# VectorE multiplies inverse sums by the gate and GpSimd applies the product; B's bias split and W_out's low parts are placed anew

## The chip, the cores and the metric

The kernel runs on one core of one Trainium2 chip. The metric is the device time of one execution in microseconds; the kernel before has a median of 1867.32 us over three runs (1866.57 to 1867.34). The engines are named as the profile names them: PE is TensorE (PEld its weight loads), DVE is VectorE, ACT is ScalarE, POOL is GpSimd, SP is SyncE, whose queue issues the DMAs.

## The reference, cut to what matters

The input is 2048 tokens of 1024 channels. One layer: an adaLN-modulated RMSNorm, one input projection, three groups of attention heads (A: 6 heads of latent attention with rotary keys; B: 5 heads over a band of chunks with a relative-position bias; C: 5 heads with a forget-gate bias), a SiLU gate on each group's output, one output projection, a gated residual and a last RMSNorm.

```
p = softmax(where(mask, s, NEG))          # s: scaled scores, plus B's or C's bias
o = p @ v                                 # per head
y = concat([a_out * silu(a_gate), b_out * silu(b_gate), c_out * silu(c_gate)]) @ w_out
x = x + gate * y
out = rmsnorm(x, final_g)
```

Everything around the change is in this form: for each head and block of 512 queries, the unnormalised output `sum exp(s) v`, the sum of the exponentials, its inverse, and the SiLU gate have to be multiplied together.

## The kernel before, in words

The tokens are worked in two halves of 1024. A half starts with a stage of projections (`stage_lv`), then runs sixteen heads in a fixed order (`order`, B0, B1, ... A5), each over two blocks of 512 queries. Values are kept to more than one fp32r term: most operands come as a high part (a copy by ACT) and a low part (a subtraction by DVE or POOL), and a product takes three matmuls.

**A tile of attention** is 128 keys by up to 512 queries. `scores` runs three matmuls into a PSUM bank `st`, and ACT takes three exponentials of it (`ph` L755, `p` L756, and `st` in place L758). `parts` lets DVE form the low part `pl = st - ph` (L764), and POOL add `p` to the running sum `acc` (L769; four buffers of `p`). `values` runs the two matmuls with `ph` and `pl` into `pv` (L778, L779), three tiles later (`LAG`).

**The end of a block** (64 of them) is `end`, `sums` and `gate`. In `end` ACT copies `pv` to `ob` (L784) and its other 64 rows to `oa` (L786); POOL adds the two halves (L787, `oa`) and multiplies `oa` by the gate `sg` (L788). `sums`, queued to come one tile step later, transposes `acc` on PE (L797), sums it on DVE (L798) and inverts it (L800, `rs`). `gate`, three steps after `end`, spreads `rs` over 512 columns with four PE transposes into a PSUM bank of the tag `mx` (L806), and DVE multiplies that bank by `oa` into `oo` (L808), which SP stores (L809). The tag `mx` has two banks and also serves the matmuls that find row maxima (L959, L970, L1040). The SBUF tag `oo` has two buffers, shared by `ob`, `oo` and the `y` of the output projection.

**The fill of a head** is a list of units that is spread over the steps of the head before it. For a B head, `bias_load` loads `te`, `tb32` and `c8`; `bias` scales them on POOL (L896 `c8`, L899 `tb32`, L900 `te`) and then makes `te`'s high part on ACT (`teh`, L903) and its low part on POOL (`tel`, L904). `evac` takes the projected queries and keys out of PSUM, ACT and DVE in turn (ACT L911, L912, L915, L916; DVE L913, L914), which frees the two banks of the tag `pj`. B0 is the first head of each half; its projections are `made` before, in the projection stage, and its fill runs at once, followed by the gate projection G0. The other eight B heads (B1 to B4 in each half) have sixteen projection units in their fill.

**The output projection** needs W_out as high and low parts in `wo`, which takes the place of the normalised input `hT` when the last gate projection has read it. `load_wo(k)` runs eight times in the second half: a 512 KB load, ACT's high part (L1063), and the low part (L1064) by DVE for even k and POOL for odd k, 128x1024 each. `out_units` then runs in the fills of the last heads.

**The order of the work.** Program order is a priority only. The framework that builds the program gives each engine an order by its own estimate of when an instruction is ready, and sets the waits between engines; each engine then runs its queue in that order and stands at the first instruction that isn't ready.

Of the kernel before, what the change touches and what calls it, by code (L numbers as in the profile page):

```python
# [8 lines left out]
F32 = mybir.dt.float32  # L9
# [4 lines left out]
ALU = mybir.AluOpType  # L14
# [47 lines left out]
def kernel(ctx: ExitStack, tc: tile.TileContext, a: dict, out: bass.AP):  # L62
    nc = tc.nc
    V, A, G, T = nc.vector, nc.scalar, nc.gpsimd, nc.tensor
    dma = nc.sync.dma_start
# [8 lines left out]
    def pst(tag, bufs=2):  # L74
        return ps.tile([128, 512], F32, tag=tag, name=tag, bufs=bufs)
# [4 lines left out]
    def wr():  # L80
        return wrp.tile([128, 1024], F32, tag="wr", name="wr", bufs=3)
# [179 lines left out]
    raw = wr()  # L261
# [466 lines left out]
    def body_units(pool, kind, tb, par, scale, qk, V_of, sg_of, dst):  # L728

        if kind == "B":  # L730
            js = [j for j in range(max(0, 4 * tb - 4), 4 * tb + 4)]
            full = 4 * tb - 1 if tb else 0
            js.remove(full)
            js = [full] + js
        else:
            js = list(range(4 * tb + 4))
        box = {}
        o0, o1 = 64 * par, 64 * par + 64
        i0, i1 = 64 - o0, 128 - o0

        def scores(n):
            j = js[n]
            d = j - 4 * tb
            if d >= 0:
                v0, v1 = 128 * d, 512
            elif kind == "B":
                v0, v1 = 0, 128 * (d + 5)
            else:
                v0, v1 = 0, 512
            c0, c1 = v0, v1  # L750
            st = pst("st", 3)
            qk(st, j, c0, c1)
            p32 = pool.tile([128, 512], F32, tag="acc" if n == 0 else "p32", name="p32", bufs=2 if n == 0 else 4)
            ph = pool.tile([128, 512], F32R, tag="ph", name="ph", bufs=PB)
            A.activation(ph[:, v0:v1], st[:, v0:v1], AF.Exp, scale=scale)  # L755
            A.activation(p32[:, v0:v1], st[:, v0:v1], AF.Exp, scale=scale)  # L756

            A.activation(st[:, v0:v1], st[:, v0:v1], AF.Exp, scale=scale)  # L758
            box[n] = (st, p32, ph, c0, c1)

        def parts(n):
            st, p32, ph, c0, c1 = box[n]
            pl = pool.tile([128, 512], F32R, tag="pl", name="pl", bufs=PB)
            V.tensor_tensor(pl[:, c0:c1], st[:, c0:c1], ph[:, c0:c1].bitcast(F32), op=ALU.subtract)  # L764
            if n == 0:
                box["acc"] = p32
            else:
                acc = box["acc"]
                G.tensor_tensor(acc[:, c0:c1], acc[:, c0:c1], p32[:, c0:c1], op=ALU.add)  # L769
            box[n] = (ph, pl, c0, c1)  # L770

        def values(n):
            if n == 0:
                box["pv"] = pst("pv", 1)
            pv = box["pv"]
            ph, pl, c0, c1 = box.pop(n)
            vt = V_of(js[n])
            T.matmul(pv[:, c0:c1], lhsT=vt, rhs=ph[:, c0:c1], start=n == 0, stop=False)  # L778
            T.matmul(pv[:, c0:c1], lhsT=vt, rhs=pl[:, c0:c1], start=False, stop=n == len(js) - 1)  # L779

        def end():
            pv = box["pv"]
            ob = pool.tile([128, 512], F32, tag="oo", name="ob", bufs=2)
            A.activation(ob, pv, AF.Copy)  # L784
            oa = pool.tile([128, 512], F32, tag="oa", name="oa", bufs=2)
            A.activation(oa[o0:o1, :], ob[i0:i1, :], AF.Copy)  # L786
            G.tensor_tensor(oa[o0:o1, :], oa[o0:o1, :], ob[o0:o1, :], op=ALU.add)  # L787
            G.tensor_tensor(oa[o0:o1, :], oa[o0:o1, :], sg_of()[o0:o1, :], op=ALU.mult)  # L788
            box["oa"] = oa


        def sums():
            acc = box["acc"]
            tp = pst("mx")
            s4 = pool.tile([128, 4], F32, tag="s4", name="s4")
            for t in range(4):
                T.transpose(tp[:, 128 * t:128 * t + 128], acc[:, 128 * t:128 * t + 128], ident)  # L797
            V.reduce_sum(s4, tp.rearrange("p (j k) -> p j k", j=4), axis=AX.X)  # L798
            rs = box["rs"] = pool.tile([128, 4], F32, tag="rs", name="rs")
            V.reciprocal(rs, s4)  # L800

        def gate():

            rb = pst("mx")
            for t in range(4):
                T.transpose(rb[:, 128 * t:128 * t + 128], box["rs"][:, t:t + 1].to_broadcast([128, 128]), ident)  # L806
            oo = pool.tile([128, 512], F32, tag="oo", name="oo", bufs=2)
            V.tensor_tensor(oo[o0:o1, :], rb[o0:o1, :], box["oa"][o0:o1, :], op=ALU.mult)  # L808
            dma(out=dst[o0:o1, :], in_=oo[o0:o1, :])  # L809

        return [(lambda n=n: scores(n), lambda n=n: parts(n), lambda n=n: values(n)) for n in range(len(js))], end, [sums, gate]

    QB, PB, LAG = 3, 3, 3
# [42 lines left out]
    class BCHead:  # L856
# [37 lines left out]
        def bias(self):  # L894
            pool, te, tb32, c8 = self.pool, self.te, self.tb32, self.c8
            G.tensor_scalar(c8, c8, 8.0, 0.0, op0=ALU.mult, op1=ALU.add)  # L896

            G.memset(tb32[:, 0:384], 0.0)
            G.tensor_scalar(tb32[:, 384:640], tb32[:, 384:640], 8.0, c8, op0=ALU.mult, op1=ALU.subtract)  # L899
            G.tensor_scalar(te, te, 8.0, c8, op0=ALU.mult, op1=ALU.subtract)  # L900
            teh = pool.tile([128, 512], F32R, tag="teh", name="teh", bufs=2)
            tel = pool.tile([128, 512], F32R, tag="tel", name="tel", bufs=2)
            A.activation(teh[:, 0:256], te, AF.Copy)  # L903
            G.tensor_tensor(tel[:, 0:256], te, teh[:, 0:256].bitcast(F32), op=ALU.subtract)  # L904
            self.teh, self.tel = teh, tel
# [22 lines left out]
        def fill(self, mid, made=None):  # L928

            grp = f"Q{self.kind}{self.h}"  # L930
            units = [] if made else [lambda: self.tiles.used(grp)]
            if self.kind == "B":
                units.append(self.bias_load)
            for n, b in enumerate(self.blocks):
                pb = made[n] if made else {}
                if not made:
                    units += proj_feat_units(self.hT, lambda: self.tiles.get(grp), b - 2 * self.half, pb)
                if n == 0 and self.kind == "B":
                    units.append(self.bias)
                units.append(lambda b=b, pb=pb: self.evac(b, pb["p"]))  # L940
                if n == 0:
                    units.append(self.load_old)
                    units += mid
            return units

        def max_units(self, b):
# [30 lines left out]
        def qk(self, b, st, j, c0, c1):  # L977
            k1, k2 = self.kb[j // 4]
            q1, q2 = self.qb[b]
            ks = slice(128 * (j % 4), 128 * (j % 4) + 128)  # L980
            d = j - 4 * b
            T.matmul(st[:, c0:c1], lhsT=k2[:, ks], rhs=q2[:, c0:c1], start=True, stop=False)  # L982
            if self.kind == "C":
                if d >= 0:
                    T.matmul(st[:, 128 * d:128 * d + 128], lhsT=ident_b, rhs=mt, start=False, stop=False)
            elif d >= -1:

                r0, r1 = max(128 * d, 0), min(128 * d + 256, 512)
                s0 = r0 - 128 * d
                T.matmul(st[:, r0:r1], lhsT=ident_r, rhs=self.teh[:, s0:s0 + r1 - r0], start=False, stop=False)  # L990
                T.matmul(st[:, r0:r1], lhsT=ident_r, rhs=self.tel[:, s0:s0 + r1 - r0], start=False, stop=False)
            T.matmul(st[:, c0:c1], lhsT=k1[:, ks], rhs=q1[:, c0:c1], start=False, stop=True)  # L992
# [67 lines left out]
    def load_wo(wo, k):  # L1060
        raw = wr()
        dma(out=raw, in_=a["w_out"][128 * k:128 * k + 128, :])
        A.activation(wo[:, 0, k, :], raw, AF.Copy)  # L1063
        (V, G)[k % 2].tensor_tensor(wo[:, 1, k, :], raw, wo[:, 0, k, :].bitcast(F32), op=ALU.subtract)  # L1064

    def out_units(pool, wo, gate, fg, i):
        b, t, box = i // 4, i % 4, {}
# [97 lines left out]
    for half in range(2):  # L1165
        if half == 0:
            made = stage_lv(0, hT, wt_pool, [h0[0][2:]] + h0[1:], lambda: h0p.__exit__(None, None, None), "QB0")
            small_loads()
            wtp.__exit__(None, None, None)
        else:  # L1170
            with opool("wt", 1) as wt_pool:
                made = stage_lv(1, hT, wt_pool, [], lambda: None, "QB0")
        KB = 4 + 2 * half
        with opool("xx") as pool:
# [40 lines left out]
            else:  # L1215
                box, fg, gate = {}, [], []
# [116 lines left out]
```

## Time and profile before

| what | value |
|---|---|
| median of three runs | 1867.32 us |
| the profiled execution, its own time | 1863.08 us |
| its span (first to last instruction) | 1861.1 us |
| mean granted TensorE clock | 0.983 of full |
| PE busy | 1714.6 us, 92% of the span |
| ACT busy | 1195.3 us, 64% |
| DVE busy | 1132.8 us, 61% |
| POOL busy | 1071.9 us, 58% |

Busy time is an average over stages with different limits. The list of waits says for each engine, line and tile how long the engine sat idle, how often and the longest time, until which instruction. In the timeline a row has its start, its length, the engine, the line, the operation, and in brackets the idle time of its engine just before it with what ended it.

### The profile page before, as it was taken

Reading aid. Unit: us, or ns where it says so; the run is one execution under the profiler, and the core shown is the slowest. Engines: PE = TensorE matmul, PEld = TensorE weight load, DVE = VectorE, ACT = ScalarE, POOL = GpSimd, SP = SyncE. Lnnn points to the kernel's source line nnn. Section 1 sums busy time; section 2 is a strip of 40 time slices with the busy share of each in tenths; the row PEclk is TensorE's granted clock in tenths of the full one; section 3 lists DMA queues with packets and bytes.
Section 4 is the critical chain, followed back from the end, with each engine's and each line's share of the span. In section 5 each row is a group of like instructions: output and inputs, shape, how many; then the busy total and the mean of one; then the engine's idle time right before and its main releaser. Section 6 shows DMA issues by size and latency. Waiting matters only on the chain.

```text
span 1861.1 us, 28271 instructions
## 1 busy us (share of the span) xinstructions
PE 1714.6 (92%) x8835; PEld 1415.7 (76%) x8835; DVE 1132.8 (61%) x2447; ACT 1195.3 (64%) x2574; POOL 1071.9 (58%) x1256
## 2 busy tenths in 40 slices
PE   3899989999999986999899999999999997999997
PEld 2799868778777754999778887777777775877786
DVE  7453547866656587344456667777777776644322
ACT  3552347678768688342357778898998887665611
POOL 1541137568655557340156666777777778787864
PEclk9999989999999999999999999999999998999999
DMA  7514845435223241144933232222332334332243
GB/s 278 166 56 149 223 137 154 124 105 186 73 77 115 63 137 46 58 133 120 249 107 95 82 89 77 75 61 76 91 99 86 88 102 129 95 113 72 71 139 113
DMA packets 139994, 209.83 MB, mean 113 GB/s; under 512 B 18734, under 2 KB 72494, under 8 KB 139764
## 3 DMA queue, kind: packets, MB, share of 16 engines
q1 hardware_dynamic: 139844, 208.03, 37.2%
q8 instruction: 70, 1.15, 0.3%
q14 instruction: 80, 0.66, 0.1%
HBM read 154.05 MB, written 57.38 MB: 114 GB/s over the span
## 4 chain that ended last, share of the span: by engine, by line
PE 41%; ACT 7%; POOL 4%; issue 3%; DVE 3%; DMA 1%; SPq 0%; ACTq 0%; DVEq 0%; POOLq 0%
PE pj L359 5%; PE pj L360 5%; PE pj L361 5%; PE pv L778 3%; PE pv L779 3%; PE st L992 2%; PE st L982 2%; ACT st L758 1%; PE mx L1040 1%; PE mx L959 1%; ACT ph L755 1%; ACT p L756 1%; PE st L1051 1%; PE st L1052 1%; POOL p L769 1%
## 5 line engine op out<-in xcount | busy, mean ns | idle before, releaser
L769 POOL TENSOR_TENSOR p<-p,p 128x512 f32<-128x512 f32 (+3 forms) x516 | 539.7, 1046 | 248.8 <-ACT p L756 206.5
L764 DVE TENSOR_TENSOR pl<-st,ph 128x512 fp32r<-128x512 f32 (+1 forms) x580 | 332.7, 576 | 200.3 <-ACT st L758 191.7
L755 ACT ACTIVATE ph<-st 128x512 fp32r<-128x512 f32 (+1 forms) x580 | 299.3, 516 | 226.8 <-PE st L992 121.6
L758 ACT ACTIVATE st<-st 128x512 f32<-128x512 f32 (+1 forms) x580 | 303.8, 524 | 0.0
L756 ACT ACTIVATE p<-st 128x512 f32<-128x512 f32 (+1 forms) x580 | 297.5, 513 | 0.7
L359 PE MATMUL pj<-hT,whi 128*128 128x512 f32 x544 | 223.5, 411 | 14.0 <-ACT q L916 14.0
L779 PE MATMUL pv<-pl,v 128*128 128x512 f32 (+1 forms) x580 | 213.9, 369 | 22.8 <-DVE pl L764 22.5
L778 PE MATMUL pv<-ph,v 128*128 128x512 f32 (+1 forms) x580 | 215.5, 372 | 10.5 <-ACT ob L784 9.8
L360 PE MATMUL pj<-hT,whi 128*128 128x512 f32 x544 | 216.8, 399 | 0.0
L361 PE MATMUL pj<-hT,wlo 128*128 128x512 f32 x544 | 216.5, 398 | 0.0
L1041 DVE TENSOR_REDUCE pm<-mx 128x1 f32<-128x512 f32 (+2 forms) x240 | 139.7, 602 | 30.0 <-PE mx L1040 28.6
L779 PEld LDWEIGHTS pv<-pl,v 128*128 128x128 f32 x580 | 110.6, 191 | 51.7 <-DVE pl L764 37.2
L778 PEld LDWEIGHTS pv<-ph,v 128*128 128x128 f32 x580 | 110.9, 191 | 39.3 <-ACT ob L784 22.6
L962 DVE TENSOR_REDUCE pm<-mx 128x1 f32<-128x512 f32 (+2 forms) x200 | 116.5, 604 | 33.5 <-PE mx L959 16.3
L787 POOL TENSOR_TENSOR oa<-oa,ob 64x512 f32<-64x512 f32 x64 | 82.7, 1292 | 82.8 <-ACT oa L786 49.7
L359 PEld LDWEIGHTS pj<-hT,whi 128*128 128x128 f32 x544 | 104.4, 192 | 28.5 <-ACT q L916 14.8
L992 PE MATMUL st<-q,k 128*128 128x512 f32 (+1 forms) x340 | 124.1, 369 | 0.7 <-DVE q L723 0.7
L982 PE MATMUL st<-q,k 128*128 128x512 f32 (+1 forms) x340 | 119.7, 352 | 1.4 <-DVE pl L764 1.0
L361 PEld LDWEIGHTS pj<-hT,wlo 128*128 128x128 f32 x544 | 103.6, 190 | 21.6
L360 PEld LDWEIGHTS pj<-hT,whi 128*128 128x128 f32 x544 | 104.2, 192 | 15.8
L1040 PE MATMUL mx<-k,q 128*128 128x512 f32 (+2 forms) x240 | 85.5, 387 | 17.3 <-DVE oo L808 8.9
L359 PE MATMUL pj<-wo,oh 128*128 128x512 f32 x256 | 101.1, 395 | 0.0
(393 smaller groups left out, 4186.6 us busy)
## 6 DMA issues: line engine op xcount, KB each, us to landing
wr<-in_w_in SPq DMA_DIRECT2D x54, 512.0 KB
wr<-in_x SPq DMA_DIRECT2D x34, 512.0 KB
v<-dva SPq DMA_DIRECT2D x36, 256.0 KB
q<-dqa SPq DMA_DIRECT2D x48, 192.0 KB
k<-dka SPq DMA_DIRECT2D x72, 128.0 KB
wa<-in_w_ada SPq DMA_DIRECT2D x16, 512.0 KB
do<-oo SPq DMA_DIRECT2D x64, 128.0 KB
wr<-do SPq DMA_DIRECT2D x128, 64.0 KB
```

What stands on the lines that cost most here:

```text
L359: T.matmul(dst, lhsT=lh, rhs=rh, start=i == 0, stop=False)
L360: T.matmul(dst, lhsT=lh, rhs=rl, start=False, stop=False)
L361: T.matmul(dst, lhsT=ll, rhs=rh, start=False, stop=i == n - 1)
L755: A.activation(ph[:, v0:v1], st[:, v0:v1], AF.Exp, scale=scale)
L756: A.activation(p32[:, v0:v1], st[:, v0:v1], AF.Exp, scale=scale)
L758: A.activation(st[:, v0:v1], st[:, v0:v1], AF.Exp, scale=scale)
L764: V.tensor_tensor(pl[:, c0:c1], st[:, c0:c1], ph[:, c0:c1].bitcast(F32), op=ALU.subtract)
L769: G.tensor_tensor(acc[:, c0:c1], acc[:, c0:c1], p32[:, c0:c1], op=ALU.add)
L778: T.matmul(pv[:, c0:c1], lhsT=vt, rhs=ph[:, c0:c1], start=n == 0, stop=False)
L779: T.matmul(pv[:, c0:c1], lhsT=vt, rhs=pl[:, c0:c1], start=False, stop=n == len(js) - 1)
L982: T.matmul(st[:, c0:c1], lhsT=k2[:, ks], rhs=q2[:, c0:c1], start=True, stop=False)
L992: T.matmul(st[:, c0:c1], lhsT=k1[:, ks], rhs=q1[:, c0:c1], start=False, stop=True)
```

## The change

1. In `end`, POOL no longer multiplies `oa` by the gate. In `gate`, DVE multiplies the spread inverse sums (PSUM) by the gate into `gr`, POOL multiplies `oa` by `gr`, and SP stores `oa` instead of `oo`.
2. The last three operations of `bias` (`teh`, `tel`) become a unit of their own, `bias_split`. For B0 of each half it comes at the end of the fill, behind both `evac`; for the other B heads before the last two projection units of the second block.
3. The low parts of W_out are all formed by POOL.

```diff
@@ body_units, end
             G.tensor_tensor(oa[o0:o1, :], oa[o0:o1, :], ob[o0:o1, :], op=ALU.add)
-            G.tensor_tensor(oa[o0:o1, :], oa[o0:o1, :], sg_of()[o0:o1, :], op=ALU.mult)
             box["oa"] = oa
@@ body_units, gate
-            oo = pool.tile([128, 512], F32, tag="oo", name="oo", bufs=2)
-            V.tensor_tensor(oo[o0:o1, :], rb[o0:o1, :], box["oa"][o0:o1, :], op=ALU.mult)
-            dma(out=dst[o0:o1, :], in_=oo[o0:o1, :])
+            gr, oa = pool.tile([128, 512], F32, tag="oo", name="gr", bufs=2), box["oa"]
+            V.tensor_tensor(gr[o0:o1, :], rb[o0:o1, :], sg_of()[o0:o1, :], op=ALU.mult)
+            G.tensor_tensor(oa[o0:o1, :], oa[o0:o1, :], gr[o0:o1, :], op=ALU.mult)
+            dma(out=dst[o0:o1, :], in_=oa[o0:o1, :])
@@ BCHead.bias
             G.tensor_scalar(te, te, 8.0, c8, op0=ALU.mult, op1=ALU.subtract)
+
+        def bias_split(self):
+            pool, te = self.pool, self.te
             teh = pool.tile([128, 512], F32R, tag="teh", name="teh", bufs=2)
             tel = pool.tile([128, 512], F32R, tag="tel", name="tel", bufs=2)
             A.activation(teh[:, 0:256], te, AF.Copy)
@@ BCHead.fill
             if self.kind == "B":
                 units.append(self.bias_load)
+                if made:
+                    units.append(self.bias)
             for n, b in enumerate(self.blocks):
                 pb = made[n] if made else {}
                 if not made:
                     units += proj_feat_units(self.hT, lambda: self.tiles.get(grp), b - 2 * self.half, pb)
-                if n == 0 and self.kind == "B":
+                if n == 0 and self.kind == "B" and not made:
                     units.append(self.bias)
                 units.append(lambda b=b, pb=pb: self.evac(b, pb["p"]))
                 if n == 0:
                     units.append(self.load_old)
                     units += mid
+            if self.kind == "B":
+                units.insert(len(units) if made else -3, self.bias_split)
             return units
@@ load_wo
-        (V, G)[k % 2].tensor_tensor(wo[:, 1, k, :], raw, wo[:, 0, k, :].bitcast(F32), op=ALU.subtract)
+        G.tensor_tensor(wo[:, 1, k, :], raw, wo[:, 0, k, :].bitcast(F32), op=ALU.subtract)
```

## Rows read from the trace of the kernel before

**Rows 1.** The page, part 1: busy us, share of the span, instructions.

```profile
PE 1714.6 (92%) x8835; PEld 1415.7 (76%) x8835; DVE 1132.8 (61%) x2447; ACT 1195.3 (64%) x2574; POOL 1071.9 (58%) x1256
```

**Rows 2.** Windows: stretch, length, busy us of PE, PEld, DVE, ACT, POOL, clock, DMA.

```profile
1180.00:1520.00 340.00, 327.48 (x1545) 251.78 (x1543) 261.76 (x469) 302.42 (x637) 254.12 (x210) 0.99 0.28 81
...
1524.00:1553.00 29.00, 17.28 (x68) 12.03 (x67) 23.57 (x31) 21.83 (x40) 24.65 (x16) 0.84 0.57 171
```

**Rows 3.** Waits, whole span, SP's own last: total us, times, longest.

```profile
DVE oo L808 <- POOL oa L788: 32.6, 13, 5.9
...
ACT teh L903 <- POOL te L900: 13.1, 3, 6.3
...
PE mx L1040 <- DVE oo L808: 8.9, 5, 2.4
...
SPq L809 <- DVE oo L808: 278.0, 53, 10.8
...
SPq L887 <- POOL tel L904: 19.1, 6, 5.3
```

**Rows 4.** Groups by line and shape: GpSimd's running sums of full tiles.

```profile
L769 POOL TENSOR_TENSOR p<-p,p 128x512 f32<-128x512 f32 x279 | 363.1, 1302 | 119.4 <-ACT p L756 97.4 <-PE pj L361 4.8 <-DVE rs L800 3.5
```

**Rows 5.** Timeline around the end of one block, 1314 to 1320 us.

```profile
1315.95 1.29 POOL L788 TENSOR_TENSOR oa<-oa,sg 64x512 f32<-64x512 f32 x1
...
1317.28 0.68 DVE L808 TENSOR_TENSOR oo<-mx,oa 64x512 f32<-64x512 f32 x1 [2.22 <-POOL oa L788]
...
1318.61 0.50 PE L779 MATMUL pv<-pl,v 128*128 128x512 f32 x1 [1.61 <-DVE pl L764]
...
1319.61 0.60 ACT L755 ACTIVATE ph<-st 128x512 fp32r<-128x512 f32 x1 [0.85 <-PE st L992]
```

**Rows 6.** Timeline, PE: first and last of nine idles behind L808.

```profile
735.67 0.50 PE L779 MATMUL pv<-pl,v 128*128 128x512 f32 x1 [3.02 <-DVE pl L764]
...
1573.83 0.50 PE L1040 MATMUL mx<-k,q 128*128 128x512 f32 x1 [1.58 <-DVE oo L808]
```

**Rows 7.** Timeline, change of halves, 741 to 747 us.

```profile
741.95 1.09 PE L806 MATMUL mx<-c_ident,rs 128*128 128x128 f32 x4 [1.35 <-DVE rs L800]
...
745.24 2.95 ACT L349 ACTIVATE wbhi<-wr 128x1024 fp32r<-128x1024 f32 x3 [2.95 <-POOL oa L788]
...
746.35 0.69 PE L359 MATMUL st<-wbhi,hT 128*128 128x384 f32 x1 [3.31 <-ACT wbhi L349]
```

**Rows 8.** Timeline, start of the heads in each half, ACT and PE.

```profile
242.59 0.59 ACT L915 ACTIVATE k<-pj 64x512 fp32r<-64x512 f32 x1
...
246.75 0.42 ACT L903 ACTIVATE teh<-te 128x256 fp32r<-128x256 f32 x1 [3.57 <-POOL te L900]
...
247.84 0.79 PE L359 MATMUL pj<-hT,whi 128*128 128x512 f32 x1 [7.45 <-ACT q L916]
...
248.43 0.63 PE L360 MATMUL pj<-hT,whi 128*128 128x512 f32 x1
...
253.42 0.39 PE L360 MATMUL pj<-hT,whi 128*128 128x512 f32 x1
...
925.58 0.59 ACT L915 ACTIVATE k<-pj 64x512 fp32r<-64x512 f32 x1
...
929.38 0.42 ACT L903 ACTIVATE teh<-te 128x256 fp32r<-128x256 f32 x1 [3.21 <-POOL te L900]
...
930.47 0.79 PE L359 MATMUL pj<-hT,whi 128*128 128x512 f32 x1 [6.54 <-ACT q L916]
```

**Rows 9.** W_out's low parts: min/median/max ns; waits from 1515 to 1560 us.

```profile
L1064 DVE TENSOR_TENSOR wo<-wr,wo x4: 1225/1779/5193, 1527.4 to 1546.3; 128x1024 fp32r<-128x1024 f32 x4
L1064 POOL TENSOR_TENSOR wo<-wr,wo x4: 2337/2418/3367, 1528.3 to 1546.8; 128x1024 fp32r<-128x1024 f32 x4
...
PE pv L779 <- DVE pl L764: 7.0, 3, 4.9
```

**Rows 10.** The bias's low part on GpSimd: min/median/max ns, first and last start.

```profile
L904 POOL TENSOR_TENSOR tel<-te,teh x10: 722/738/744, 247.3 to 1047.8; 128x256 fp32r<-128x256 f32 x10
```

## The prediction

> **What bounds the kernel now.** I read the busy shares first. PE is busy 92% of the span and no other engine over 64% [rows 1], so time is to be had only where PE stands still. Second, the windows: from 1180 to 1520 us, in the second half's heads, PE is busy 327.5 of 340 us and ACT 302.4 [rows 2]. PE loses 12.5 us there, and ACT, 89% busy, is close behind: a PE idle that goes is worth nearly its length, unless ACT's exponentials then set the pace. Third, the list of waits, looking for waits that the changed lines make [rows 3]: DVE stands 32.6 us in 13 places at L808 until POOL's gate product L788, ACT stands 13.1 us at `teh` until POOL's `te`, and the matmuls of the row maxima wait 8.9 us for L808 to free its `mx` bank. Last, the timeline of PE, to see which of these waits leave PE idle, since only that counts.
>
> **The epilogue.** Instruction counts and shapes stay: one DVE and two POOL products of 64x512 per block, 64 blocks. What changes is the order. Now POOL does L787, often one running sum of 1.30 us [rows 4], then L788 of 1.29 us; DVE stands at L808 with `pl` of later tiles queued behind it. In [rows 5] DVE stands 2.22 us, PE then 1.61 us for `pl`, and ACT 0.85 us for PE. Afterwards DVE's product needs the spread sums and the gate, and both are there earlier; POOL's second product waits for DVE instead. In the timeline of PE I find nine idles of this kind after 700 us, between 3.02 and 1.45 us, together 16.9 us; [rows 6] has the first and the last. Full length is the upper end; the lower end is the ratio at ACT, 0.85/1.61, hence 9.0 us. I take three quarters, 12.7 us, because PE is the fuller engine in rows 2 but not by much. At the change of halves ACT's first weight part waits until 745.24 for L788, the last reader of the gate whose memory it takes; with the change DVE's product, 0.68 us behind the transposes that end at 743.04, is that reader, so ACT starts near 743.8: 1.4 us [rows 7]. The sum is 14.1 us, from 9.0 to 18.3.
>
> What this adds: POOL's product waits for DVE, and behind it on POOL stand the running sums, whose four `p` buffers let ACT go on for four tiles. The store now leaves after POOL, about one product (1.29 us) after DVE's. SP already stands 278 us in total at this store [rows 3], with loads of later heads behind it; a store 1.3 us later would be hidden by loads that run a head ahead, and where POOL was late anyway it isn't later at all. I cost it at nothing; without that cover it would be up to 64 x 1.3 us of load delay, on the path only where a head starts on a load.
>
> **The two starts.** Before each half's heads, PE waits for a `pj` bank that ACT frees with L916. ACT stands at `teh` in between, because POOL's `te` waits for the load of `c8`. L915 ends at 243.18, yet L916 follows `teh` at 247.20; without `teh` it starts there, 4.0 us earlier, and in the second half 926.17 instead of 929.82, 3.6 us earlier [rows 8]. Together 7.6 us. The lower end is half, 3.8 us, if other ScalarE work slides in. After each idle, matmuls are spaced 0.43 us until 253.1, at the 1.2 GHz level, instead of 0.23 at 2.4 GHz [rows 8]; twelve matmuls, so 2.4 us per start. The idles that remain are 3.4 and 2.9 us; one of 3.31 us was followed by the low level [rows 7], one of 3.02 us was not [rows 6]. Between two such rows I count no gain and put 4.8 us on the upper end: 12.4 us.
>
> **The bias's split for the other eight heads** keeps its work, ACT 0.42 us and POOL 0.74 us [rows 8, 10], but comes as the third unit before the end of a fill, so that `tel` has only some projections of cover before the first scores read it. With room in its order it costs nothing; at worst PE waits for one running sum and `tel`, 1.30 + 0.74 = 2.0 us a head [rows 4, 10], 16 us in all. I take an eighth, 2 us: `te` is ready long before, so both can be put in any gap. The next `te` load, which already holds SP 19.1 us behind `tel` [rows 3], will come later too; eight projection units lie between that load and its use, so I cost it at nothing.
>
> **W_out's low parts.** DVE's four take 1.23 to 5.19 us, 10.0 us together, POOL's four 2.4 us each [rows 9]. PE waits 7.0 us for `pl` in that stretch [rows 9], 4.9 of it behind the part of 5.19 us. That goes. POOL gets four more of 2.42 us, 9.7 us, into a stretch in which it is busy 24.65 of 29 us [rows 2]; 4.35 us are free, so POOL falls 5.3 us behind, and the four `p` buffers hold back about that much, 4 x 1.30 us. I take half of the 5.3 us as lost: 7.0 - 2.7 = 4.3 us. The ends are 7.0 - 5.3 - 5.3 = -3.6 us, if later `wr` loads wait as well, and 7.0 + 2.4 = 9.4 us, if a low clock level goes too. The Trainium skill, GPSIMD Engine Reference, section 4.1 on engine selection, advises against two-input elementwise work on GpSimd and puts it at about twice VectorE's time. By that rule the four parts lose 4 x (2.42 - 1.78) = 2.6 us by the medians, and the sum below is 17 us instead of 24; the trace agrees with its direction, but one of DVE's four took 5.19 us beside GpSimd's work, which the rule leaves out.
>
> **The sum** is 14.1 + 7.6 + 4.3 - 2 = 24 us. The profiled execution took 1863.1 us (2.0 us around its span), 4.2 us under the median of 1867.3 us. It becomes 1839 us, and against the median 1843 us.
>
> **The rivals.**
>
> *GpSimd is the limit around W_out.* POOL's order puts the low parts ahead of the running sums; ACT stands for `p`, and PE for ACT. Then that part gives -3.6 instead of 4.3 us, and the late buffers hold up two block ends of the next head, 2 us: 1867.3 - 14.1 - 7.6 + 2 + 3.6 + 2 = 1853 us. For it: POOL is 85% busy there. Against: the loads pace the eight parts. The rule cited above points to this case.
>
> *ScalarE takes over.* At 89% busy [rows 2] ACT may hide most of the epilogue's gain: 4 us of it, the starts 7.6 us, W_out and the split nothing, 1 us at the halves, so 1855 us. Against it: ACT itself idles behind PE in [rows 5].
>
> *The order shifts.* The framework reorders every queue; other small waits of PE take the place of those removed, and only 0 to 3 us remain: about 1866 us.
>
> *GpSimd's queue stops at the gate product: slower.* If the framework places POOL's product early, POOL stands while the sums go through PE, DVE, PE and DVE, at least 1.09 + 0.68 us for the last two [rows 5, 7], with running sums behind it; L808's wait comes back on another engine. It decides from the point where POOL falls four `p` buffers, 5.2 us, behind: then ACT stops. At 0.6 us a block on the path, a third of these 1.77 us, it is 38 us over 64 blocks against the 24 us gained: 1867.3 + 14 = 1881 us. For it: POOL is busy 254 of 340 us [rows 2]. Against: in [rows 5] DVE waited last for POOL and not for the sums, so there nothing would stand.
>
> **How the numbers follow.** Chances: the forecast 0.52, GpSimd around W_out 0.12, ScalarE 0.14, the order 0.09, GpSimd's queue 0.13. About 0.2%, 3.7 us, is what a measurement of this kernel can tell from no change. Faster is 0.52 + 0.12 + 0.14 = 0.78, the same 0.09, slower 0.13. All upper ends together give 18.3 + 12.4 + 9.4 = 40 us, 1827 us; all lower ones 9.0 + 3.8 - 3.6 - 16 = -7 us, 1874 us. For 8 in 10 I take 1829 to 1867 us: it holds the forecast without its last corners, both faster rivals and the case of the order.
>
> **What would show it.** Right: no wait of DVE at the new gate product for POOL, PE's idles of [rows 6] gone, PE's first matmul of the heads 4.0 and 3.6 us nearer to the one before it, no L1064 on DVE, and PE's wait for `pl` near 1550 us gone. Wrong: POOL idle before its product until DVE for more than 0.5 us a block, ACT idle at `p` behind POOL, PE idle at the matmuls with `teh` or `tel`, or PE's idle time unchanged with other names.

## The result, and the profile of the changed kernel

The changed kernel takes 1841.07 us (median of four runs, 1836.47 to 1842.21) against 1866.94 us (1865.56 to 1867.34): a ratio of 0.9867, with an interval of 0.9854 to 0.9881, or 25.9 us less. Forecast were 1843 us and 24 us less. The size is right, and partly by luck: the experiments show two terms that were wrong in opposite directions.

First the page of the changed kernel, part 1 (columns as in rows 1):

```profile
PE 1715.8 (93%) x8835; PEld 1415.0 (77%) x8835; DVE 1125.4 (61%) x2443; ACT 1195.2 (65%) x2574; POOL 1079.8 (59%) x1260
```

Busy times hardly move against [rows 1]: 7.4 us leave DVE and 7.9 come to POOL. The profiled span fell by 20.7 us, to 1840.4 us (the execution's own time is 1842.21 us), so the time came out of idle stretches. The list of waits, SP's own last (columns as in rows 3; the gate product on DVE is now `gr` L807, the product on POOL L808, the running sums' transposes L796, the row maxima L1047):

```profile
ACT teh L906 <- POOL te L900: 10.8, 4, 6.4
...
PE pv L779 <- DVE pl L764: 9.3, 13, 1.8
...
PE mx L796 <- POOL p L769: 9.2, 7, 3.0
...
POOL oa L808 <- PE st L1059: 7.1, 2, 3.6
...
POOL oa L808 <- DVE gr L807: 2.2, 5, 0.7
...
DVE gr L807 <- POOL oa L787: 0.9, 1, 0.9
...
SPq L809 <- POOL oa L808: 358.2, 61, 12.4
```

DVE's 32.6 us of standing at the product [rows 3] are 0.9 us, and POOL's new wait for DVE is 2.2 us in five of 64 blocks. Two more places belong to it, though the list gives them to PE: POOL stands 3.5 us before the products at 474.71 and 724.55, and both times DVE's product ended 0.08 us earlier (473.95 + 0.68, 723.79 + 0.68). That makes 9.3 us in seven blocks. At the second of these POOL had stood 2.77 us before the change too, at the running sum at 726.66, for want of the next `p`. PE's wait for `pl` fell from 22.5 us in 18 places to 9.3 in 13, and the 8.9 us until `oo` freed an `mx` bank [rows 3] are 0.6. New is the third line: PE stands 9.2 us for POOL's running sums, where it stood 2.1 us before. The timeline of the changed kernel has each step:

```profile
243.13 0.79 PE L359 MATMUL pj<-hT,whi 128*128 128x512 f32 x1 [3.45 <-ACT q L919]
243.72 0.63 PE L360 MATMUL pj<-hT,whi 128*128 128x512 f32 x1
...
439.97 1.06 ACT L175 ACTIVATE sq<-wr 128x1024 f32<-128x1024 f32 x1 [4.50 <-DMA wr<-in_x]
...
744.22 0.69 PE L359 MATMUL st<-wbhi,hT 128*128 128x384 f32 x1 [1.99 <-ACT wbhi L349]
...
925.42 0.80 PE L359 MATMUL pj<-hT,whi 128*128 128x512 f32 x1 [2.89 <-ACT q L919]
926.01 0.63 PE L360 MATMUL pj<-hT,whi 128*128 128x512 f32 x1
...
1304.21 0.67 DVE L807 TENSOR_TENSOR gr<-mx,sg 64x512 f32<-64x512 f32 x1
...
1306.77 1.28 POOL L787 TENSOR_TENSOR oa<-oa,ob 64x512 f32<-64x512 f32 x1 [0.83 <-ACT oa L786]
...
1309.27 1.29 POOL L808 TENSOR_TENSOR oa<-oa,gr 64x512 f32<-64x512 f32 x1
...
1510.58 7.06 POOL L1071 TENSOR_TENSOR wo<-wr,wo 128x1024 fp32r<-128x1024 f32 x3
...
1517.58 1.27 POOL L769 TENSOR_TENSOR p<-p,p 128x256 f32<-128x256 f32 x2
...
1518.38 1.00 PE L796 MATMUL mx<-c_ident,p 128*128 128x128 f32 x2 [1.87 <-POOL p L769]
...
1543.54 0.47 PE L796 MATMUL mx<-c_ident,p 128*128 128x128 f32 x1 [3.03 <-POOL p L769]
```

The block end near 1305 us is the plainest case: DVE is through with its product at 1304.88, before POOL has even begun the sum L787. In the old order DVE would have stood until past 1309. At the two starts PE's idle is 3.45 and 2.89 us, where it was 7.45 and 6.54 [rows 8], and at the change of halves 1.99 instead of 3.31 us [rows 7]. From 1510 us on the new cost shows: three low parts of W_out back to back hold POOL for 7.06 us, the running sum stands behind them, and PE waits 1.87 us for it, later 3.03 us.

To compare kernels stage by stage, the table takes a matmul that runs 64 times in every kernel, the transpose of the padded maxima (L722). Its 57th and 63rd run (56 and 62 counted from 0) start at 1480.22 and 1672.26 us before and at 1464.89 and 1652.20 after; W_out lies between them. Each entry is the time between two such runs, in one profiled execution. (Two expectations below call them, loosely, the first sums' transpose of a block end; this is the stretch meant.)

| kernel | to 0 | 0–12 | 12–14 | 14–28 | 28–32 (second start) | 32–48 | 48–56 | 56–62 (W_out) | 62–end |
|---|---|---|---|---|---|---|---|---|---|
| before | 264.8 | 165.0 | 27.3 | 224.5 | 268.6 | 331.9 | 198.1 | 192.0 | 188.8 |
| after | 260.2 | 165.7 | 31.4 | 223.1 | 265.0 | 330.0 | 189.4 | 187.3 | 188.2 |
| after, again | 263.1 | 165.8 | 27.2 | 223.1 | 262.9 | 330.0 | 189.5 | 186.8 | 188.1 |
| epilogue alone | 264.0 | 166.1 | 28.3 | 223.4 | 268.0 | 331.3 | 189.3 | 181.2 | 188.1 |
| bias alone | 259.5 | 167.3 | 27.3 | 225.0 | 264.0 | 331.0 | 198.2 | 192.1 | 188.8 |
| W_out alone | 265.8 | 167.3 | 28.5 | 225.2 | 268.7 | 331.8 | 201.1 | 189.3 | 188.9 |
| after, W_out on both | 261.1 | 165.6 | 28.0 | 223.2 | 261.9 | 330.5 | 189.4 | 182.0 | 188.1 |
| after, W_out on DVE | 262.0 | 165.7 | 28.5 | 223.4 | 263.8 | 330.5 | 189.5 | 182.1 | 188.1 |
| the same again | 262.7 | 166.0 | 28.5 | 223.1 | 266.8 | 330.0 | 189.5 | 180.6 | 188.2 |

Two columns carry most of the gain. 48–56 is 189.3 to 189.5 us in every kernel of the table with the new epilogue and over 198 in the three without it. 56–62 falls into three groups: 192 before, 187 with W_out on POOL, 181 to 182 with the new epilogue and W_out as before or on DVE. "After, again" and "the same again" repeat the program of the row that they follow or name, and so show how far one stage varies by itself: 4.2 us in 12–14, up to 3 us at either start.

### The profile page after: what moved, and what is told of

It is laid out like the page before. It is cut to its first block, busy times and chain, and to the rows that moved or that the text cites. A ratio compares the mean times of both kernels' runs of the same rounds, so it can differ in the third digit from the quotient of the medians.

```text
span 1840.4 us, 28356 instructions
## 1 busy us (share of the span) xinstructions
PE 1715.8 (93%) x8835; PEld 1415.0 (77%) x8835; DVE 1125.4 (61%) x2443; ACT 1195.2 (65%) x2574; POOL 1079.8 (59%) x1260
## 4 chain that ended last, share of the span: by engine, by line
PE 67%; ACT 10%; issue 7%; DVE 6%; POOL 6%; DMA 3%; SPq 0%; ACTq 0%; DVEq 0%; POOLq 0%
PE pj L359 9%; PE pj L361 9%; PE pj L360 9%; PE pv L778 5%; PE pv L779 5%; PE st L999 3%; PE st L989 2%; ACT st L758 2%; PE mx L966 2%; ACT p L756 2%; PE mx L1047 2%; ACT ph L755 2%; PE st L360 2%; PE st L359 2%; PE st L1057 2%
## 5 line engine op out<-in xcount | busy, mean ns | idle before, releaser
L787 POOL TENSOR_TENSOR oa<-oa,ob 64x512 f32<-64x512 f32 x64 | 82.6, 1291 | 68.6 <-ACT oa L786 37.3
L361 PE MATMUL pj<-wo,ol 128*128 128x512 f32 x256 | 100.1, 391 | 0.7 <-POOL ol L1084 0.7
## 6 DMA issues: line engine op xcount, KB each, us to landing
q<-dqa SPq DMA_DIRECT2D x48, 192.0 KB
```

The costliest lines, as they stand in the source:

```text
L361: T.matmul(dst, lhsT=ll, rhs=rh, start=False, stop=i == n - 1)
```

## The experiments

**1. The epilogue alone** (part 1 of the change, in the kernel before):

```diff
-            G.tensor_tensor(oa[o0:o1, :], oa[o0:o1, :], sg_of()[o0:o1, :], op=ALU.mult)
...
-            V.tensor_tensor(oo[o0:o1, :], rb[o0:o1, :], box["oa"][o0:o1, :], op=ALU.mult)
+            V.tensor_tensor(gr[o0:o1, :], rb[o0:o1, :], sg_of()[o0:o1, :], op=ALU.mult)
+            G.tensor_tensor(oa[o0:o1, :], oa[o0:o1, :], gr[o0:o1, :], op=ALU.mult)
```

> The kernel before with the first part of the change alone: DVE multiplies the spread sums by the gate, POOL the output by that; the bias's split and W_out's low parts stay as before. Theory (DVE's wait for POOL was PE's idle, 9 places): about 14 us faster than before, 9 to 18, most of it after 1300 us; the idles of PE behind DVE's product are gone. Rival (ScalarE then sets the pace): 4 to 6 us faster, with ScalarE's busy share near 100% in the second half's heads. Rival (the wait comes back as PE's wait for POOL's running sums): under 4 us faster, PE idle at the transposes of the running sum up by as much as the old idles were.

Measured: 1842.03 us against 1864.69, ratio 0.9878 (0.9863 to 0.9893): 22.7 us, nearly the whole of the change and more than the 9 to 18 us expected. The table puts 8.8 us of it in 48–56 and 10.8 us in 56–62. The windows of these two stretches (columns as in rows 2; the clock is the granted share of 2.4 GHz), first of the kernel before, then of this one:

```profile
1282.13:1480.22 198.09, 189.70 (x893) 146.50 (x892) 152.57 (x275) 175.44 (x373) 149.20 (x124) 0.99 0.30 88
1480.22:1672.26 192.04, 172.50 (x765) 134.93 (x763) 125.72 (x211) 142.75 (x288) 150.49 (x131) 0.96 0.38 113
```

```profile
1281.02:1470.35 189.33, 187.39 (x892) 145.35 (x891) 152.93 (x275) 174.75 (x373) 147.61 (x123) 1.00 0.31 92
1470.35:1651.53 181.18, 168.66 (x765) 132.71 (x763) 122.31 (x212) 142.90 (x288) 151.97 (x132) 0.99 0.40 120
```

The same matmuls (within one) take 2.3 and 3.8 us less time on PE, at a granted clock of 1.00 and 0.99 instead of 0.99 and 0.96; the rest, 6.5 and 7.0 us (8.4 to 1.9, 19.5 to 12.5), is time in which PE was not busy. So up to about 6 of the 19.6 us come by the clock, which fell less once the idles were shorter; a matmul right after an idle also counts longer (0.50 instead of 0.39 us in the timelines below), and the two were not taken apart. And two timelines answer a question on W_out, which this kernel leaves as it was, first that of the kernel before, then this one's:

```profile
1545.68 0.68 DVE L808 TENSOR_TENSOR oo<-mx,oa 64x512 f32<-64x512 f32 x1 [2.94 <-POOL oa L788]
1546.29 5.19 DVE L1064 TENSOR_TENSOR wo<-wr,wo 128x1024 fp32r<-128x1024 f32 x1
...
1552.13 0.80 PE L779 MATMUL pv<-pl,v 128*128 128x512 f32 x1 [4.88 <-DVE pl L764]
```

```profile
1531.24 0.67 DVE L807 TENSOR_TENSOR gr<-mx,sg 64x512 f32<-64x512 f32 x1
1531.84 1.21 DVE L1064 TENSOR_TENSOR wo<-wr,wo 128x1024 fp32r<-128x1024 f32 x1
```

This low part, DVE's fourth, is the one that took 5.19 us before [rows 9]. There it began right behind an L808 that had stood 2.94 us for POOL, and ran beside POOL's own part and running sums; here the product does not stand, and the part takes 1.21 us. So the epilogue alone takes away the 4.9 us of PE that hung on it, and leaves W_out's move nothing to gain there.

**2. The bias alone** (part 2 of the change):

```diff
+                if made:
+                    units.append(self.bias)
...
-                if n == 0 and self.kind == "B":
+                if n == 0 and self.kind == "B" and not made:
...
+            if self.kind == "B":
+                units.insert(len(units) if made else -3, self.bias_split)
```

> The kernel before with the second part alone: the split of the bias into high and low part comes at the end of the first head's fill, and for the other eight B heads two projection units before the end. Theory: 7.6 us come from the two starts (PE's first matmul of each half's heads 4.0 and 3.6 us earlier) and the late split costs 2 us: 5 to 6 us faster than before. Rival (the late split of the other eight heads costs as much as the starts give): 0 to 3 us faster; the 4 us that the changed kernel loses between the heads A0 and B2 of the first half show here too.

Measured: 1855.53 us, ratio 0.9948 (0.9933 to 0.9963): 9.2 us, above the 5 to 6 expected. The table has 5.3 us at the first start and 4.6 at the second. The 2.3 us that 0–12 grew by need not be the late split's: the next kernel, which leaves the bias as it was, has the same 167.3. The timeline of this kernel at the first start:

```profile
243.45 0.50 PE L359 MATMUL pj<-hT,whi 128*128 128x512 f32 x1 [3.45 <-ACT q L919]
243.78 0.39 PE L360 MATMUL pj<-hT,whi 128*128 128x512 f32 x1
```

The idle is the 3.45 us of the changed kernel, but the second matmul takes 0.39 us, not 0.63: the granted clock of the next 6 us is 1.00 (2.4 GHz) here and 0.54 in the changed kernel.

**3. W_out alone** (part 3 of the change):

```diff
-        (V, G)[k % 2].tensor_tensor(wo[:, 1, k, :], raw, wo[:, 0, k, :].bitcast(F32), op=ALU.subtract)
+        G.tensor_tensor(wo[:, 1, k, :], raw, wo[:, 0, k, :].bitcast(F32), op=ALU.subtract)
```

> The kernel before with the third part alone: all eight low parts of W_out on POOL. Theory: PE's 7.0 us of waits for DVE's low part of the scores go and POOL's lag takes back 2.7 us: about 4 us faster. Rival (POOL is the limit there): 4 us slower, with PE waiting for POOL's running sums in that stretch. Rival (the DVE part of 5.19 us was slow only because of POOL at its side, and its removal pays twice): 7 to 9 us faster.

Measured: 1864.01 us, ratio 0.9992 (0.9979 to 1.0004): no change, and none of the three expectations. In its own stretch 2.7 us go; in 48–56, where its work does not lie, 3.0 us come. These are busy time of PE (192.8 instead of 189.7 us) at a granted clock of 0.97 instead of 0.99, with no more idle, in a profiled execution that was the slowest of the ten (1868.51 us). The wait for `pl` behind the 5.19 us part is gone, but its timeline shows what replaces it:

```profile
1535.55 7.04 POOL L1064 TENSOR_TENSOR wo<-wr,wo 128x1024 fp32r<-128x1024 f32 x3 [0.58 <-ACT wo L1063]
...
1543.33 0.33 PE L797 MATMUL mx<-c_ident,p 128*128 128x128 f32 x1 [1.54 <-POOL p L769]
```

**4. The old products, with the gate unit five steps behind the block's end instead of three.** It gives POOL more time, but DVE's product still takes its operand from POOL.

```diff
-                    tail.extend((clock[0] + d, u) for d, u in zip((1, 3), t))
+                    tail.extend((clock[0] + d, u) for d, u in zip((1, 5), t))
```

> The kernel before with one number changed: the unit that spreads the inverse sums and multiplies (DVE) and stores comes five tile steps after a block's end instead of three. No operation changes its engine or order of factors. Theory (only DVE's standing for POOL's gate product costs): POOL is through by then, most of the nine idles go, 8 to 14 us faster than before. Rival (what helps is that DVE's product takes no operand of POOL at all, since POOL lags in any step): less than 4 us faster. Rival (the store or the last block's chain then comes too late): slower by about two tile steps, 4 us, at the ends of the halves.

Measured: 1858.12 us, ratio 0.9957 (0.9940 to 0.9974): 6.6 us, under a third of experiment 1, between the 8 to 14 us of the theory and the rival's 4. Its list of waits:

```profile
PE pv L779 <- DVE pl L764: 28.5, 22, 3.0
DVE oo L808 <- POOL oa L788: 25.8, 9, 5.9
```

DVE still stands 25.8 of the 32.6 us, the longest 5.9 us as before: where it stood longest, two further steps were not enough. Part of the shortfall may be the later store: 62–end is 191.0 us here instead of 188.8. So two steps of slack do not give the epilogue's gain, and an order in which DVE takes no operand from POOL does; more slack was not tried.

**5. The changed kernel, with the later eight B heads splitting right behind the bias**, as before the change; only the starts split late.

```diff
-                    units.append(self.bias)
+                    units += [self.bias, self.bias_split]
...
-            if self.kind == "B":
-                units.insert(len(units) if made else -3, self.bias_split)
+            if self.kind == "B" and made:
+                units.append(self.bias_split)
```

> The changed kernel, with the late split kept only for the first head of each half; the other eight B heads form the low part right behind the bias, as before. Theory (the late split by itself costs the 2 us that the kernel with the split alone lost between the blocks at 313 and 375 us): 1 to 3 us faster than the changed kernel, about 1839 us. Rival (those 2 us come with any order of the first heads and the late split is free): the same as the changed kernel within 1 us, 1841 us.

Measured: 1842.86 us, ratio 0.9881 (0.9856 to 0.9905) to a median before of 1863.98. That is the changed kernel's ratio, with an interval too wide to exclude 2 us by itself. By stretches the late split of these eight costs nothing: outside 12–14 and the starts, which vary by themselves, no stretch of this kernel is over 0.7 us shorter than the changed kernel's (166.4 us in 0–12, 223.4 in 14–28, 331.6, 189.5, 186.6 and 188.0 from 32 on). The rival of this run held.

**6 to 8. W_out put back.** Three kernels from the changed one: low parts on DVE and POOL in turn (6), the same with experiment 5's edit (7), all on DVE (8, `V` in place of `(V, G)[k % 2]`).

```diff
-        G.tensor_tensor(wo[:, 1, k, :], raw, wo[:, 0, k, :].bitcast(F32), op=ALU.subtract)
+        (V, G)[k % 2].tensor_tensor(wo[:, 1, k, :], raw, wo[:, 0, k, :].bitcast(F32), op=ALU.subtract)
```

> The changed kernel with W_out's low parts on DVE and POOL in turn, as before: the first two parts of the change. Theory (with the epilogue rearranged, POOL is late in that stretch and its four extra parts cost what the epilogue's change gained there: 7 us less was won between the blocks at 1480 and 1590 us than with the epilogue alone): about 1834 us, 7 us faster than the changed kernel, with PE's waits for POOL's running sums near 1518 and 1543 us (1.87 and 3.03 us) gone. Rival (those waits only change their names, since DVE's parts then hold up the low part of the scores): 1839 to 1842 us.

> Both: the late split at the two starts alone, and W_out's low parts on DVE and POOL in turn. If both theories hold and add up: 1831 to 1833 us, the fastest so far. If the first falls: like the kernel with W_out on both alone. If the second falls: like the one with the starts alone.

> The changed kernel with all eight low parts of W_out on DVE. Theory (POOL is the limit in that stretch, DVE has room once it stands for nobody): as fast as with both engines or faster, 1832 to 1836 us, each part 1.2 to 1.9 us on DVE. Rival (a DVE part beside POOL's work stretches to several us and holds up the scores' low parts): 1840 us or slower, PE waiting over 5 us more for DVE's low part of the scores between 1500 and 1560 us.

Measured: 1835.35 us, ratio 0.9848 (0.9825 to 0.9870); 1838.80, 0.9860 (0.9839 to 0.9882); 1835.32, 0.9847 (0.9832 to 0.9861). Their 56–62 are 182.0, 182.1 and 182.1 us against 187.3. Experiments 5 and 7 differ in W_out's parts alone: 186.6 against 182.1 us in the stretch, 1842.86 against 1838.80 us in all, with overlapping intervals. So the move of W_out to POOL costs some 5 us in its stretch once the epilogue is changed. Run 7 missed the 1831 to 1833 us expected if both theories held; the first of them had failed in run 5. DVE takes all eight parts in run 8 in the same 182.1 us, though not without a price: PE stands behind three of them in a row (4.22 us from 1508.72), where in run 6 it stands 1.57 us.

```profile
1513.72 0.79 PE L1059 MATMUL st<-q,k 128*128 128x512 f32 x1 [4.35 <-DVE q L723]
```

**9. The squares of x one step later**, in kernel 6. I had put down the 4 us that the changed kernel loses between runs 12 and 14 of L722 to ScalarE's wait for a load of x (4.50 us at 439.97 in the timeline above).

```diff
-                mids[7] = mids.get(7, []) + [lambda t=t: x_norm(load_x(8 + t, wr()), pool.tile([128, D], F32, tag="xn", name="sq", bufs=3),
+                mids[8] = mids.get(8, []) + [lambda t=t: x_norm(load_x(8 + t, wr()), pool.tile([128, D], F32, tag="xn", name="sq", bufs=3),
```

> The changed kernel with W_out's low parts on both engines, and the eight x_norm units of a head put one step later. Theory (the wait of ScalarE's square for the x load, 2.6 us near 440 us in the run with both engines and 4.5 us in the changed kernel, is part of what the first start gained and lost again): no such wait of ScalarE over 1 us, and 1 to 4 us less than with both engines alone, 1831.5 to 1834.5 us. Rival (the wait only moves to the next piece of work that reads the load, or the later units crowd what follows them): 1835 to 1838 us, with a wait of PE in the next 100 us that is not in the other runs.

Measured: 1840.18 us, ratio 0.9874 (0.9855 to 0.9894), 5 us more than kernel 6 (whose interval overlaps) and beyond the rival's 1838. The wait moved, to the next loads of the same kind:

```profile
460.49 1.06 ACT L175 ACTIVATE sq<-wr 128x1024 f32<-128x1024 f32 x1 [3.21 <-DMA wr<-in_x]
...
464.82 0.80 PE L778 MATMUL pv<-ph,v 128*128 128x512 f32 x1 [2.44 <-ACT ob L784]
```

The rival held as to the wait: 14–28 grew from 223 to 230.8 us. Of that, 6.3 us are busy time of PE (221.3 us at a granted clock of 0.96, where the changed kernel's second execution has 215.0 at 1.00). The next run takes the theory's ground away.

**10 and 11. The changed kernel again, and W_out on DVE again, side by side.** The instruction order of these two is the same on every engine up to the loads and parts of W_out, so the 5.7 us between kernel 8 and the result could be the spread of runs.

> The changed kernel as it is, beside the next one on one chip. Theory (W_out's low parts on GpSimd cost about 5 us once the epilogue is changed): 1840 to 1843 us, and 186 to 188 us for the stretch from the first sums' transpose of the 56th to that of the 62nd block end. Rival (the 5.7 us to the kernel with DVE forming them are the spread of runs, since both kernels are the same up to 1530 us): 1836 to 1838 us, within 2 us of the next one.

> The changed kernel with all of W_out's low parts on VectorE, a second time, beside the changed kernel on one chip. Theory: 4 to 6 us under the changed kernel of the same call, 1834 to 1837 us, and 181 to 183 us for the same stretch. Rival: within 2 us of it.

Measured: 1838.72 us, ratio 0.9875 (0.9860 to 0.9890), and 1837.92 us, 0.9866 (0.9850 to 0.9882). By the whole time the two can't be told apart, as the rival had it. By the stretch they can: 186.8 against 180.6 us, as the theory had it, and no kernel with the new epilogue and W_out's parts on DVE or on both lies above 182.1 there, apart from the 184.8 of run 9. What hid it in these two executions is elsewhere: the second start, 262.9 us in the first and 266.8 in the second, in code that is the same. The timeline of the changed kernel's second execution there:

```profile
924.77 0.50 PE L359 MATMUL pj<-hT,whi 128*128 128x512 f32 x1 [2.90 <-ACT q L919]
925.11 0.39 PE L360 MATMUL pj<-hT,whi 128*128 128x512 f32 x1
```

After an idle of 2.90 us the matmuls go on at 0.39 us; in the first execution of the same program, after 2.89 us, at 0.63 (timeline above, 926.01). The trace of run 11 has the low level there as well. The same second execution has 27.2 us in 12–14, as before the change, with a wait of 1.8 us for x instead of 4.5, so the loss of 4 us near 440 us is not fixed to the program. It came in two more executions (30.7 us in 12–14 with a wait of 3.75 us in run 5, 31.1 with 4.15 in run 7); what decides it stays open.

How the cost of W_out on POOL divides shows in the windows of 56–62, of the changed kernel's two executions and of run 11:

```profile
1464.89:1652.20 187.31, 173.34 (x765) 135.59 (x764) 116.99 (x208) 143.18 (x288) 158.17 (x136) 0.95 0.38 116
...
1461.62:1648.45 186.83, 171.96 (x764) 134.78 (x763) 117.01 (x208) 143.08 (x288) 158.21 (x136) 0.96 0.38 116
...
1466.53:1647.17 180.64, 167.00 (x765) 132.59 (x764) 126.34 (x216) 142.84 (x288) 142.91 (x128) 0.99 0.40 120
```

PE's idle is 14.0 and 14.9 us with the parts on POOL and 13.6 in run 11; the rest of the difference is PE's busy time at a lower granted clock. Over all nine executions with the new epilogue the three with W_out on POOL have 14.0 to 14.9 us of idle and 172.0 to 173.3 us busy, the six others 11.5 to 13.6 and 167.0 to 172.3. By the means that is 1.8 us of idle and 3.0 us of busy time. Run 9 has the 172.3 us, at 0.96 with 12.6 us of idle, where kernel 6, the same in this stretch, has 169.0 at 0.98 with 13.0: the busy time varies by itself by some 3 us.

The view by line of run 11 (min/median/max ns, first and last start) prices the low parts on DVE:

```profile
L1071 DVE TENSOR_TENSOR wo<-wr,wo x8: 1210/1218/1742, 1511.9 to 1529.6; 128x1024 fp32r<-128x1024 f32 x8
```

and that of the changed kernel on POOL:

```profile
L1071 POOL TENSOR_TENSOR wo<-wr,wo x8: 2360/2388/2435, 1510.6 to 1533.1; 128x1024 fp32r<-128x1024 f32 x8
```

The Trainium skill, GPSIMD Engine Reference, section 4.1 on engine selection, puts two-input elementwise work on GpSimd at about twice VectorE's time; 2388 to 1218 ns is 1.96, so the traces agree.

## Why the prediction was right, and where it was not

**What bounds the kernel: right.** Every microsecond gained is PE idle or PE at the low clock level; no other engine took over. In 48–56 ACT stays at 175 us busy while the stretch shrinks by 8.7 us, so ScalarE did not set the pace and that rival falls.

**The epilogue: right in mechanism, mis-sized.** Forecast were 12.7 us from nine idles; the two stretches of experiment 1 gave 19.6. Two things are missing from the term. The 4.9 us behind the 5.19 us low part were read as W_out's, because the wait's last releaser was `pl` behind that part; one step further back stood L808, which had held DVE, and without that stand the part was short. And no clock was counted, though the profile had the stretch at 0.84 [rows 2]: up to about 6 us. The 13.5 us of idle that went are not the 12.7 of the term. Four of the nine idles, 6.8 us, lie in 48–56, where 6.5 us went: nearly full length, so there the three quarters taken because of ACT, 89% busy, were caution that ACT did not call for. Three more, 5.5 us, lie in 56–62 with the 4.9 us, and 7.0 of these 10.3 went. The first of the nine, 3.02 us at the end of the first half [rows 6], came back in large part under other names: in experiment 1 PE waits there 2.07 us for `pl`, where it waited 1.01 at 728.88, and 1.41 us for the running sum.

```profile
730.27 0.80 PE L1050 MATMUL st<-q,k 96*128 96x512 f32 x1 [2.07 <-DVE pl L764]
...
738.33 0.33 PE L796 MATMUL mx<-c_ident,p 128*128 128x128 f32 x1 [1.41 <-POOL p L769]
```

The 1.4 us at the change of halves measured 1.3 as PE idle. (The lower end given as 9.0 us is 16.9 x 0.85/1.61 = 8.9 and leaves these 1.4 out.)

**What the epilogue adds: nearly right.** POOL stands 9.3 us in seven places for DVE's product, 0.15 us a block, so the slower rival, POOL's queue stopping at the product, hardly happened. SP does stand longer at the store, 358.2 us instead of 278.0 [rows 3], and it was costed at nothing. PE now waits 1.6 us in two places for a load of `df` (L966), which it never did before and does in experiment 1 too (1.7 us); that the store is what delays this load was not tried.

**The two starts: right.** Forecast 4.0 and 3.6 us, measured as PE idle 4.00 and 3.65. The clock was left out between two rows that spoke for and against it, and that was as much as could be known: in nine executions with an idle of 2.89 or 2.90 us at the second start, the granted clock of the following 6 us was 1.00 in four, 0.72 in three and 0.50 or 0.51 in two. With the 3.45 us at the first start it was 1.00 in one, 0.76 in two, 0.50 to 0.54 in six. The Trainium skill, TensorE: Matmul & The Clock Gate, Part 1, states that the number of slow matmuls at a kernel's start varies from run to run of one kernel. The two executions of the changed kernel show the like after a pause in its middle, 0.50 after 2.89 us and 1.00 after 2.90.

**The late split of eight heads:** -2 us forecast, no cost found in any stretch (experiment 5).

**W_out: wrong, and this is the step that failed.** It read: PE waits 7.0 us for `pl`, "4.9 of it behind the part of 5.19 us. That goes", less half of POOL's lag, +4.3 us. All 7.0 us were credited, though only 4.9 stood behind that part; in the changed kernel PE still waits 3.1 us for `pl` from 1500 to 1545 us. (POOL's parts were put at 2.4 us each; one of the four took 3.37 [rows 9].) Alone it measured no change, with 2.7 us gained in its stretch. In the company of the epilogue there was nothing left to gain, since the part of 5.19 us was 1.21 already, and the move to POOL cost: 181.2 us in the stretch with the epilogue alone, 187.3 and 186.8 with the whole change, so 5.6 to 6.1 us lost. That this is near the lag worked out in the prediction, 5.3 us, is chance: PE's idle grew by 1.5 and 2.4 us, and 4.7 and 3.3 are PE's busy time at a granted clock of 0.95 and 0.96 instead of 0.99. The rival that GpSimd is the limit around W_out had the mechanism right (PE waits for `p`, 1.87 and 3.03 us in the timeline); its 1853 us failed mainly because the epilogue gave more than forecast and the split cost nothing.

**The sum.** By stretches it is 19.6 + 1.3 for the epilogue and the change of halves, 7.65 for the starts, 0 for the split and about -5.9 for W_out: 22.7 us. The spans fell by 20.7 and 24.5 us in the two profiled executions, the medians by 25.9 and 24.3. The forecast of 24 us came from 6.8 us too little for the epilogue and the halves, 2 too little for the split, and 10.2 too much for W_out; what is left between 22.7 and the measured figures is of the size by which one stage varies. Experiments 1 to 3 add up to 22.7 + 9.2 + 0.7 = 32.6 us, more than the whole change: the parts overlap at W_out, where two of them remove the same wait and one then adds its own.

**The better version** is likely the change with W_out's low parts kept off POOL alone: on DVE, or on both engines as before. The kernel with W_out on DVE has a median of 1835.7 us (experiments 8 and 11, eight runs, 1834.86 to 1839.30), the changed kernel 1839.9 (the result and experiment 10, eight runs, 1836.47 to 1842.21). But the kernel before moved too, from 1866.94 us beside the result to 1863.98 and 1862.97 beside the experiments, and side by side (experiments 10 and 11) the two were 0.8 us apart with overlapping intervals. So a gain of about 5 us is seen in its stretch, more than half of it as busy time at a lower clock, and on the whole time it is likely and not shown.

## What to carry to other kernels

When an in-order engine that feeds TensorE takes an operand from a slower engine, let the two change places: the fast engine multiplies the operands that are there early, the slow one does the last step that only a store waits for. A wait belongs to what made its releaser late: before crediting an edit with a wait, follow the releaser's own queue one instruction back, and ask whether another part of the change already moves that. And compare kernels stretch by stretch, between two runs of one instruction, where whole times differ by less than they scatter; and split each stretch into idle and busy time, since the clock can make up most of a difference.

## What the runs showed of the hardware

I had not expected that idles of equal length end differently: 2.89 us before the low clock level in one execution of a program, 2.90 us before the full level in another; the 28–32 column of these two differs by 2.1 us. Nor that a subtraction of 128x1024 on DVE takes 5.19 us in one place and 1.21 us in another. Both ran beside POOL, the first beside a low part and two running sums, the second beside running sums; which overlap stretches it was not tried by itself.
